# Down projections of two feed-forward layers as seven block products in place of eight, on one Trainium2 core

## The chip, the cores and the metric

The kernel runs on one core of a Trainium2 chip. The core has five engines with queues of their own: TensorE (PE, matmul), VectorE (DVE), ScalarE (ACT), GpSimd (POOL) and SyncE (SP, which here issues the transfers). The metric is the device time of one execution in microseconds (us), as the median of the runs.

## What is computed

A backbone block of two layers over 512 latent tokens (x) and 256 context tokens (ctx), width 1024, in float32. Each layer is attention in three head groups, then a SwiGLU feed-forward with 2816 hidden columns. Layer 1, the last, computes the latent tokens alone. The part that matters, shortened:

```python
def swiglu(h, w1, w3, w2):
    return (jax.nn.silu(h @ w1) * (h @ w3)) @ w2

for layer in range(2):
    last = layer == 1
    ...                                   # modulation mx, mc of c and c_ctx; attention
    x = x + mx[5] * swiglu(modulate(rmsnorm(x, g_ffn[layer]), mx[3], mx[4]),
                           w_ff1[layer], w_ff3[layer], w_ff2[layer])
    if not last:
        ctx = ctx + mc[5] * swiglu(modulate(rmsnorm(ctx, g_ffn[layer]), mc[3], mc[4]),
                                   w_ff1[layer], w_ff3[layer], w_ff2[layer])
return rmsnorm(x, g_final)
```

## The kernel before

Every operation is recorded first (`Plan`, `_Queue`), then a planner lists them by priority and due time and issues them, so that each engine has one fixed order of instructions; all of them carry the line of the issuing call, L375. An operation recorded on `act_dve` or `dve_pool` may go to either of two engines, as the planner decides. `LEAD` says how far ahead weights are asked for, and the buffers of each tag in `SLOTS` set how far ahead they can be: "u" has 39 buffers of 4 KB per partition, for weights, hidden columns, sums and operands alike; "pt" (8) and "s" (7) are the probability and score buffers of attention, "T" is four PSUM buffers of 512 columns and "S" two of a block's up projection.

A float32 matmul is made of three in float32r: each operand is split into a high part (a copy that rounds) and a low part (the operand less its high part), and hi·hi, hi·lo and lo·hi add up in PSUM. For weights `split_w` loads `ws` from HBM and makes `wh` and `wl`.

The feed-forward takes the hidden columns in 22 blocks `ft` of 128. `ff_up` multiplies w1 and w3 of a block with the normalized tokens (hx 512 columns, hc 256): 24 matmuls of 512 columns for each of w1 and w3, and in layer 0 another 24 of 256 columns. ScalarE takes silu of the first into `sg`; `ff_gate` multiplies by the second and splits into `gh` and `gl`. The down projection `ff_down` of block ft - 1 stands between the up parts of block ft: per tile of 128 tokens two halves of 512 output columns with three matmuls each, into two "T" buffers, which DVE adds into the accumulator `y` of that tile (`ys`; six tiles in layer 0, four in layer 1). The last FF_TAIL = 3 blocks are kept back and done after the loop (label ffE), where their products add up in PSUM and go to x through the gate. In layer 0 the loop also carries the modulation of layer 1 (`ada_later`, FF_ADA): DVE operations scalar_tensor_tensor into `acc`, from weights `wa`.

Of the kernel before, what the change touches and what calls it, by code (L numbers as in the profile page):

```python
# [12 lines left out]
F32R = mybir.dt.float32r  # L13
AF = mybir.ActivationFunctionType
ALU = mybir.AluOpType
# [13 lines left out]

ORDER = ["dddd P0 P1 ddddB P2 BABeeeeABAeeeeBABABABeeeeeeeeeCAAAACCCCCC",  # L30
         "P1 P0 B P2 ABBBCAACAABCCCAAB"]
FF_TAIL = 3
FF_ADA = "dddd"
PV_RUN = {"A": 3, "B": 3, "C": 2}
QK_AHEAD = 238
# [3 lines left out]
FT = DFF // 128  # L39
# [339 lines left out]
def dit_block(  # L379
# [8 lines left out]
    plan = Plan(nc, (  # L388
        x, c, ctx_in, c_ctx, w_ada, b_ada, g_attn, g_ffn, w_in, g_q, g_k, lam_q1, lam_k1, lam_q2, lam_k2,
        g_subln, sink_logit, w_out, w_ff1, w_ff3, w_ff2, g_final, k_ident, k_mask, k_ones, k_ropeA, k_ropeB, out))  # L390
    act, dve, pe, pool, sp = (plan.queue(e) for e in ("act", "dve", "pe", "pool", "sp"))
# [14 lines left out]
    def new(tag, shape, name, dt=F32):  # L406
        return plan.tile(pools[tag], [128] + list(shape), dt, tag, nm(name))

    def U(shape, dt=F32, name="u"):
        return new("u", shape, name, dt)  # L410
# [7 lines left out]
    def PT():  # L418
        return new("T", [512], "T")
# [7 lines left out]
    def f(ap):  # L427
        return ap.bitcast(F32)

    def sub(eng, o, a, b):  # L430
        eng.tensor_tensor(o, a, b, ALU.subtract)
# [154 lines left out]
    def ada_later():  # L586
        yield from ada_run(0, (5,), (0, 1))
        yield from ada_run(1, range(2), (0, 1))
        yield from ada_run(1, range(2, 6), (0,))
# [83 lines left out]
    for l in range(2):  # L673
        last = l == 1
# [631 lines left out]
        def ff_gate(hs, sg):  # L1306
            dve.tensor_tensor(sg[:, :ncol], sg[:, :ncol], hs[:, :ncol], ALU.mult)
            gh = new("u", [768], "gh", F32R)
            act_dve.copy(gh[:, :ncol], sg[:, :ncol])
            gl = new("u", [768], "gl", F32R)  # L1310
            sub(dve, gl[:, :ncol], sg[:, :ncol], f(gh[:, :ncol]))
            return gh, gl

        def ff_w2(ft, scale=None):
            def load2(st):
                sp.dma_start(st, w_ff2[l, 128 * ft:128 * ft + 128, :])
            return split_w(load2, [1024], scale=scale)
# [14 lines left out]
        def halves(ap):  # L1332
            return [ap[:, 512 * hf:512 * hf + 512] for hf in range(2)]

        ys, gs, ada = {}, [], ada_later()
        for ft in range(FT):
            plan.label = f"ffn{l}"
            plan.lead = LEAD["else"] if ft == 0 else LEAD["ff"]
            ws = ff_weights(ft)
            down = 0 < ft <= FT - FF_TAIL  # L1340
            w2 = ff_w2(ft - 1) if down else None
            for ch in FF_ADA if l == 0 and 1 < ft < FT - FF_TAIL else "":
                plan.label, plan.lead, ada_eng[0] = "ada1", LEAD["ada"], ch
                next(ada, None)
            plan.label = f"ffn{l}"
            hs = []
            if ft == 0:
                hs = [PS(), PS()]
                for part in (2, 3) if last else (1, 2, 3):
                    for a in range(2):  # L1350
                        ff_up(ws[a], hs[a], part)
            for a in range(2):
                if ft:
                    hs.append(PS())
                s = hs[a]
                for part in range(1 if last else 2):
                    if ft:
                        ff_up(ws[a], s, part)
                    if down:
                        k = 2 * a + part  # L1360
                        for r, i in qtiles[2 * a:2 * a + 2] if last else qtiles[FF_CUT[k]:FF_CUT[k + 1]]:
                            if ft == 1:
                                ys[r, i] = U([1024], name="y")
                            for p, yv in zip(ff_down(gs, [w2], r, i), halves(ys[r, i])):
                                if ft == 1:
                                    act_dve.copy(yv, p)
                                else:
                                    dve.tensor_tensor(yv, p, yv, ALU.add)
                if a == 0:
                    sg = new("u", [768], "sg")  # L1370
                    act.activation(sg[:, :ncol], s[:, :ncol], AF.Silu)
            gs = (gs if ft > FT - FF_TAIL else []) + [ff_gate(hs[1], sg)]
        for _ in ada if not last else ():
            raise ValueError("a part of the modulation is left")
        plan.lead = LEAD["else"]
# [1 line left out]
        gates = [gate_read(l, 1, r) for r in range(1 if last else 2)]  # L1377

        gated = [(slice(512 * hf, 512 * hf + 512), gates[0][hf]) for hf in range(2)] if last else None
        w2s = [ff_w2(ft, gated) for ft in range(FT - FF_TAIL, FT)]  # L1380
        for r, i in qtiles:
            xt = xt0[r, i] = U([1024], name="xf")
            sp.dma_start(xt, xscr[NX * r + i])
            for xv, yv, gate in zip(halves(xt), halves(ys[r, i]), gates[r]):
                dve_pool.tensor_tensor(yv, yv, gate, ALU.mult)
                dve_pool.tensor_tensor(xv, xv, yv, ALU.add)
        if not last:
            hT = new_hT()
        else:
# [90 lines left out]
```

## Time and profile before

| what | value |
|---|---|
| runs | 1730.92, 1727.18, 1730.82 us |
| median | 1730.82 us |
| the profiled execution | 1727.9 us |
| its span | 1726.1 us |
| PE, DVE, ACT, POOL busy | 1677.6, 1189.7, 617.2, 128.9 us |
| granted clock of PE, mean | 0.995 |

The span is what the trace covers; the execution's own time has 1.8 us around it. Busy time is the union of an engine's instructions; matmuls overlap one another in the trace, so the distance between their starts tells more than their length.

### The profile page before, as it was taken

To read this page: it belongs to the slowest core of one execution; us is meant where nothing else is said; L and a number is where in the kernel's file an instruction comes from. 1 tells how busy PE (TensorE), PEld (TensorE's weight loads), DVE (VectorE), ACT (ScalarE), POOL (GpSimd) and SP (SyncE) were. 2 spreads that over 40 slices of the span, in tenths; PEclk is the share of its full clock that TensorE was granted. 3 is DMA by queue.
4 is the path that set the end of the run, shared out by engine and by line. 5 is a ranking of instruction groups with operands and counts; after the bars stand their busy time and mean duration, and the time that the engine had idled before them with its cause. 6 is when DMAs were issued, how large, how long until landed. Compare 5 with 4: busy or idle time off the path is not lost.

```text
span 1726.1 us, 24221 instructions
## 1 busy us (share of the span) xinstructions
PE 1677.6 (97%) x9426; PEld 1367.1 (79%) x9426; DVE 1189.7 (69%) x2036; ACT 617.2 (36%) x1278; POOL 128.9 (7%) x167
## 2 busy tenths in 40 slices
PE   7999898999999999999999999999999999999998
PEld 4787676777888888888888888777777888888886
DVE  3766978576568877676645775787776666666676
ACT  2523877663431212112111153267674411111111
POOL 0230200010000000000000001232000000000010
PEclk9999999999999999999999999999999999999999
DMA  9502230334352555345133251022006632332441
GB/s 322 184 31 85 68 86 1 117 89 120 114 179 86 171 171 168 102 158 164 44 91 117 98 171 37 25 50 50 1 2 164 177 110 74 110 107 77 122 146 49
DMA packets 153278, 182.96 MB, mean 106 GB/s; under 512 B 9316, under 2 KB 121396, under 8 KB 153164
## 3 DMA queue, kind: packets, MB, share of 16 engines
q1 hardware_dynamic: 153164, 181.42, 34.0%
q8 instruction: 74, 1.21, 0.3%
q14 instruction: 40, 0.33, 0.1%
HBM read 163.00 MB, written 9.47 MB: 100 GB/s over the span
## 4 chain that ended last, share of the span: by engine, by line
PE 87%; DVE 5%; ACT 3%; DMA 3%; issue 1%; SPq 1%; POOL 0%; DVEq 0%; POOLq 0%; ACTq 0%
DMA ws__2963<-in_w_out_dram 1%; SPq L375 1%; DMA ws__2951<-in_w_out_dram 1%; PE S__1380 L375 1%; PE S__1379 L375 1%; PE S__1756 L375 0%; PE S__1628 L375 0%; PE S__1561 L375 0%; PE S__1881 L375 0%; PE S__1691 L375 0%; PE S__1823 L375 0%; PE S__1495 L375 0%; PE S__1995 L375 0%; PE S__1993 L375 0%; PE S__1984 L375 0%
## 5 line engine op out<-in xcount | busy, mean ns | idle before, releaser
L375 POOL TENSOR_TENSOR y__1397<-y__1397,gate__1998 128x512 f32<-128x512 f32 x1 | 1.3, 1294 | 481.7 <-DVE y__1397 L375 481.7
L375 POOL TENSOR_TENSOR ws__3494<-ws__3494,gate__3489 128x512 f32<-128x512 f32 x1 | 1.3, 1304 | 292.6 <-DMA ws__3494<-in_w_ff_dram 292.6
L375 DVE TENSOR_TENSOR wl__2186<-ws__2184,wh__2185 128x1024 fp32r<-128x1024 f32 x1 | 1.2, 1224 | 11.6 <-PE T__2121 L375 11.6
L375 ACT ACTIVATE sg__1468<-S__1461 128x768 f32<-128x768 f32 x1 | 0.8, 812 | 21.2 <-PE S__1461 L375 21.2
L375 ACT ACTIVATE sg__1966<-S__1959 128x768 f32<-128x768 f32 x1 | 0.8, 812 | 21.2 <-PE S__1959 L375 21.2
L375 ACT ACTIVATE sg__1860<-S__1853 128x768 f32<-128x768 f32 x1 | 0.8, 812 | 21.2 <-PE S__1853 L375 21.2
L375 ACT ACTIVATE sg__1914<-S__1907 128x768 f32<-128x768 f32 x1 | 0.8, 812 | 21.2 <-PE S__1907 L375 21.2
L375 ACT ACTIVATE sg__1940<-S__1933 128x768 f32<-128x768 f32 x1 | 0.8, 812 | 21.2 <-PE S__1933 L375 21.2
L375 ACT ACT_TABLE_LOAD x6 | 7.7, 1283 | 0.8 <-PEq L1465 0.7
L375 POOL TENSOR_TENSOR ropeG<-ropeA,gqk 128x64 f32<-128x64 f32 (+1 forms) x10 | 6.5, 673 | 5.9 <-DVE gqk L375 5.9
L375 DVE TENSOR_TENSOR sg__1994<-sg__1994,S__1995 128x768 f32<-128x768 f32 x1 | 1.0, 954 | 8.4 <-PE S__1995 L375 8.4
L375 ACT ACTIVATE xn__2033<-xf__2011 128x1024 f32<-128x1024 f32 x1 | 1.1, 1061 | 14.2 <-DVE xf__2011 L375 14.2
L375 PE MATMUL T__115<-wa__116,cstat 128*32 128x128 f32 x8 | 0.7, 417 | 5.6 <-DMA wa__116<-in_w_ada_dram 5.6
L375 ACT ACTIVATE sg__1994<-S__1993 128x768 f32<-128x768 f32 x1 | 0.8, 812 | 14.7 <-PE S__1993 L375 14.7
L375 ACT ACTIVATE sg__3107<-S__3102 128x512 f32<-128x512 f32 x1 | 0.6, 598 | 14.8 <-PE S__3102 L375 14.8
L375 ACT ACTIVATE sg__3195<-S__3190 128x512 f32<-128x512 f32 x1 | 0.6, 597 | 13.9 <-PE S__3190 L375 13.9
L375 ACT ACTIVATE sg__3305<-S__3300 128x512 f32<-128x512 f32 x1 | 0.6, 597 | 13.9 <-PE S__3300 L375 13.9
L375 ACT ACTIVATE sg__3415<-S__3410 128x512 f32<-128x512 f32 x1 | 0.6, 597 | 13.9 <-PE S__3410 L375 13.9
L375 ACT ACTIVATE sg__3129<-S__3124 128x512 f32<-128x512 f32 x1 | 0.6, 597 | 13.9 <-PE S__3124 L375 13.9
L375 ACT ACTIVATE sg__3239<-S__3234 128x512 f32<-128x512 f32 x1 | 0.6, 597 | 13.9 <-PE S__3234 L375 13.9
L375 ACT ACTIVATE sg__3151<-S__3146 128x512 f32<-128x512 f32 x1 | 0.6, 597 | 13.8 <-PE S__3146 L375 13.8
L375 ACT ACTIVATE sg__3261<-S__3256 128x512 f32<-128x512 f32 x1 | 0.6, 597 | 13.8 <-PE S__3256 L375 13.8
(14006 smaller groups left out, 6608.3 us busy)
## 6 DMA issues: line engine op xcount, KB each, us to landing
x__83<-in_x_dram SPq DMA_DIRECT2D x1, 512.0 KB
x__84<-in_x_dram SPq DMA_DIRECT2D x1, 512.0 KB
x__131<-in_x_dram SPq DMA_DIRECT2D x1, 512.0 KB, 5.9
x__136<-in_x_dram SPq DMA_DIRECT2D x1, 512.0 KB, 6.5
x__198<-in_ctx_dram SPq DMA_DIRECT2D x1, 512.0 KB
x__203<-in_ctx_dram SPq DMA_DIRECT2D x1, 512.0 KB
ws__241<-in_w_in_dram SPq DMA_DIRECT2D x1, 512.0 KB
ws__244<-in_w_in_dram SPq DMA_DIRECT2D x1, 512.0 KB
```

The costliest lines, as they stand in the source:

```text
L375: getattr(self.real[op.eng], method)(*args, **kw)
```

## The change

In each layer the blocks 0 to 17 are taken in nine pairs. The hidden columns of a pair (two blocks of 128) and w2's two blocks make a product of 2x2 blocks: the tokens are cut into two halves (384 each in layer 0, 256 in layer 1), the inner dimension into the pair's two blocks, w2's columns into two halves of 512. `wino_down` forms four sums of activations (S) and four of w2 (T) on DVE, splits each operand into high and low parts (`fh`, `fl`), and makes seven products in place of eight, each with an accumulator `yw` per tile of tokens; they stand as a generator between the up parts of the next two blocks. `wino_sum` adds the accumulators up into the four quarters after the loop. 21 accumulators of 2 KB in layer 0 and 14 in layer 1 take the place of six and four `y` of 4 KB; HOMES puts 12 and 10 of them into "pt" and "s" buffers, the others lie in "u". The tail is four blocks in place of three, the gate operations after the loop are on DVE alone, and the multiply by `hs` of a pair's blocks is no longer followed by a split of its own.

```diff
--- before.py
+++ after.py
@@ -29,7 +29,9 @@
 
 ORDER = ["dddd P0 P1 ddddB P2 BABeeeeABAeeeeBABABABeeeeeeeeeCAAAACCCCCC",
          "P1 P0 B P2 ABBBCAACAABCCCAAB"]
-FF_TAIL = 3
+FF_TAIL = (4, 4)
+WINO = (0, 1)
+HOMES = ({'pt': 8, 's': 4}, {'pt': 6, 's': 4})
 FF_ADA = "dddd"
 PV_RUN = {"A": 3, "B": 3, "C": 2}
 QK_AHEAD = 238
@@ -1332,14 +1334,120 @@
         def halves(ap):
             return [ap[:, 512 * hf:512 * hf + 512] for hf in range(2)]
 
+        def split_s(src, shape):
+            hi = U(shape, F32R, "fh")
+            act_dve.copy(hi, src)
+            lo = U(shape, F32R, "fl")
+            sub(dve, lo, src, f(hi))
+            return hi, lo
+
+        spare = []
+
+        def wino_home(form, t):
+
+            for tag, n in HOMES[l].items():
+                if homes.get(tag, 0) < n and (tag != "pt" or form in (1, 5, 6)):
+                    homes[tag] = homes.get(tag, 0) + 1
+                    return new(tag, [512], "yw")
+            if not spare:
+                y = U([2, 512], name="yw")
+                spare.extend((y[:, 1], y[:, 0]))
+            return spare.pop()
+
+        def wino_down(Ge, Go, ft, first):
+
+
+            n = ncol // 2
+            nt = n // 128
+            raws2 = []
+            for k in range(2):
+                w = U([1024], name="w2")
+                sp.dma_start(w, w_ff2[l, 128 * (ft + k):128 * (ft + k) + 128, :])
+                raws2.append(w)
+            we, wo2 = raws2
+            a11, a21, a12, a22 = Ge[:, 0:n], Ge[:, n:2 * n], Go[:, 0:n], Go[:, n:2 * n]
+            b11, b12, b21, b22 = we[:, 0:512], we[:, 512:1024], wo2[:, 0:512], wo2[:, 512:1024]
+
+            def product(form, A, B):
+                (ah, al), (bh, bl) = A, B
+                y = None
+                for t in range(nt):
+                    c = slice(128 * t, 128 * t + 128)
+                    p = PT()
+                    with plan.together():
+                        for k, (a, b) in enumerate(((ah, bh), (ah, bl), (al, bh))):
+                            pe.matmul(p, lhsT=a[:, c], rhs=b, start=(k == 0), stop=(k == 2))
+                    if first:
+                        wino_y[form, t] = wino_home(form, t)
+                        act_dve.copy(wino_y[form, t], p)
+                    else:
+                        dve.tensor_tensor(wino_y[form, t], p, wino_y[form, t], ALU.add)
+
+            def pair(h, j):
+                return h[0][:, j], h[1][:, j]
+
+            sa = split_s(a11, [n])
+            sb = split_s(b11, [512])
+            product(1, sa, sb)
+            yield
+            S, T = U([2, n], name="S12"), U([2, 512], name="T12")
+            dve.tensor_tensor(S[:, 0], a21, a22, ALU.add)
+            sub(dve, T[:, 0], b12, b11)
+            sub(dve, S[:, 1], S[:, 0], a11)
+            sub(dve, T[:, 1], b22, T[:, 0])
+            s12, t12 = split_s(S, [2, n]), split_s(T, [2, 512])
+            S3, T3 = U([2, n], name="S34"), U([2, 512], name="T34")
+            sub(dve, S3[:, 0], a11, a21)
+            sub(dve, T3[:, 0], b22, b12)
+            sub(dve, S3[:, 1], a12, S[:, 1])
+            sub(dve, T3[:, 1], T[:, 1], b21)
+            product(5, pair(s12, 0), pair(t12, 0))
+            yield
+            product(6, pair(s12, 1), pair(t12, 1))
+            yield
+            s34, t34 = split_s(S3, [2, n]), split_s(T3, [2, 512])
+            product(7, pair(s34, 0), pair(t34, 0))
+            yield
+            so2 = split_s(wo2, [1024])
+            so2 = [h.rearrange("p (j n) -> p j n", j=2) for h in so2]
+            product(3, pair(s34, 1), pair(so2, 1))
+            yield
+            sgo = split_s(Go[:, 0:2 * n], [2 * n])
+            sgo = [h.rearrange("p (j n) -> p j n", j=2) for h in sgo]
+            product(4, pair(sgo, 1), pair(t34, 1))
+            yield
+            product(2, pair(sgo, 0), pair(so2, 0))
+            yield
+
+        def wino_sum():
+
+            nt = ncol // 256
+            for t in range(nt):
+                y = [None] + [wino_y[form, t] for form in range(1, 8)]
+                dve.tensor_tensor(y[2], y[1], y[2], ALU.add)
+                dve.tensor_tensor(y[6], y[1], y[6], ALU.add)
+                dve.tensor_tensor(y[7], y[6], y[7], ALU.add)
+                dve.tensor_tensor(y[6], y[6], y[5], ALU.add)
+                dve.tensor_tensor(y[3], y[6], y[3], ALU.add)
+                sub(dve, y[4], y[7], y[4])
+                dve.tensor_tensor(y[7], y[7], y[5], ALU.add)
+                ys[tiles[t]] = [y[2], y[3]]
+                ys[tiles[nt + t]] = [y[4], y[7]]
+
+        homes = {}
+        wino_y, wino, G = {}, None, []
+        tail = FF_TAIL[l]
         ys, gs, ada = {}, [], ada_later()
         for ft in range(FT):
             plan.label = f"ffn{l}"
             plan.lead = LEAD["else"] if ft == 0 else LEAD["ff"]
             ws = ff_weights(ft)
-            down = 0 < ft <= FT - FF_TAIL
+            down = 0 < ft <= FT - tail and l not in WINO
+            if l in WINO and 0 < ft <= FT - tail and ft % 2 == 0:
+                wino = wino_down(*G, ft - 2, ft == 2)
+                G = []
             w2 = ff_w2(ft - 1) if down else None
-            for ch in FF_ADA if l == 0 and 1 < ft < FT - FF_TAIL else "":
+            for ch in FF_ADA if l == 0 and 1 < ft < FT - tail else "":
                 plan.label, plan.lead, ada_eng[0] = "ada1", LEAD["ada"], ch
                 next(ada, None)
             plan.label = f"ffn{l}"
@@ -1366,10 +1474,22 @@
                                     act_dve.copy(yv, p)
                                 else:
                                     dve.tensor_tensor(yv, p, yv, ALU.add)
+                    for _ in range(2 if last else 1):
+                        next(wino, None) if wino else None
                 if a == 0:
                     sg = new("u", [768], "sg")
                     act.activation(sg[:, :ncol], s[:, :ncol], AF.Silu)
-            gs = (gs if ft > FT - FF_TAIL else []) + [ff_gate(hs[1], sg)]
+            if l in WINO and ft < FT - tail:
+                dve.tensor_tensor(sg[:, :ncol], sg[:, :ncol], hs[1][:, :ncol], ALU.mult)
+                G.append(sg)
+            else:
+                gs = (gs if ft > FT - tail else []) + [ff_gate(hs[1], sg)]
+        if wino:
+            for _ in wino:
+                pass
+            wino_sum()
+        else:
+            ys = {k: halves(y) for k, y in ys.items()}
         for _ in ada if not last else ():
             raise ValueError("a part of the modulation is left")
         plan.lead = LEAD["else"]
@@ -1377,13 +1497,13 @@
         gates = [gate_read(l, 1, r) for r in range(1 if last else 2)]
 
         gated = [(slice(512 * hf, 512 * hf + 512), gates[0][hf]) for hf in range(2)] if last else None
-        w2s = [ff_w2(ft, gated) for ft in range(FT - FF_TAIL, FT)]
+        w2s = [ff_w2(ft, gated) for ft in range(FT - tail, FT)]
         for r, i in qtiles:
             xt = xt0[r, i] = U([1024], name="xf")
             sp.dma_start(xt, xscr[NX * r + i])
-            for xv, yv, gate in zip(halves(xt), halves(ys[r, i]), gates[r]):
-                dve_pool.tensor_tensor(yv, yv, gate, ALU.mult)
-                dve_pool.tensor_tensor(xv, xv, yv, ALU.add)
+            for xv, yv, gate in zip(halves(xt), ys[r, i], gates[r]):
+                dve.tensor_tensor(yv, yv, gate, ALU.mult)
+                dve.tensor_tensor(xv, xv, yv, ALU.add)
         if not last:
             hT = new_hT()
         else:
```

**The order of PE,** in layer 1, at the start of a down projection. Names: `T` the PSUM buffer, `wh`, `wl` and `gh`, `gl` the parts of w2 and of the activations, `fh`, `fl` those of the operands of a product. Before, one tile pair of a block:

```order
L375 MATMUL T__3241<-wh__3232,gh__3223 128x512
L375 MATMUL T__3242<-wh__3232,gh__3223 128x512
L375 MATMUL T__3241<-wl__3233,gh__3223 128x512
L375 MATMUL T__3242<-wl__3233,gh__3223 128x512
L375 MATMUL T__3241<-wh__3232,gl__3224 128x512
L375 MATMUL T__3242<-wh__3232,gl__3224 128x512
L375 MATMUL T__3243<-wh__3232,gh__3223 128x512
L375 MATMUL T__3244<-wh__3232,gh__3223 128x512
L375 MATMUL T__3243<-wl__3233,gh__3223 128x512
```

Now, products 1 and 5 of a pair:

```order
L377 MATMUL T__3373<-fh__3371,fh__3369 128x512
L377 MATMUL T__3373<-fl__3372,fh__3369 128x512
L377 MATMUL T__3373<-fh__3371,fl__3370 128x512
L377 MATMUL T__3374<-fh__3371,fh__3369 128x512
L377 MATMUL T__3374<-fl__3372,fh__3369 128x512
L377 MATMUL T__3374<-fh__3371,fl__3370 128x512
L377 MATMUL T__3383<-fh__3379,fh__3377 128x512
L377 MATMUL T__3383<-fl__3380,fh__3377 128x512
L377 MATMUL T__3383<-fh__3379,fl__3378 128x512
L377 MATMUL T__3384<-fh__3379,fh__3377 128x512
L377 MATMUL T__3384<-fl__3380,fh__3377 128x512
L377 MATMUL T__3384<-fh__3379,fl__3378 128x512
```

Each product has three matmuls to a buffer of 512 columns, all of one buffer together, where the two halves of a tile alternated before.

**The order of DVE,** in layer 0, from the gate multiply on in the middle of the modulation's work (blocks 4 and 5). Names: `sg` the activations, `y` and `yw` the accumulators, `acc` the modulation, `w` a block of w2, `S` and `T` without a PSUM operand the sums. Before:

```order
L375 TENSOR_TENSOR sg__1532<-sg__1532,S__1533 128x768
L375 TENSOR_TENSOR y__1408<-T__1536,y__1408 128x512
L375 TENSOR_TENSOR y__1408<-T__1537,y__1408 128x512
L375 TENSOR_TENSOR gl__1541<-sg__1532,gh__1540 128x768
L375 TENSOR_TENSOR y__1411<-T__1538,y__1411 128x512
L375 TENSOR_TENSOR y__1411<-T__1539,y__1411 128x512
L375 SCALAR_TENSOR_TENSOR acc__1557<-wa__1560,cstat,acc__1557 128x1024
L375 COPY cols__1554<-T__1553 128x16
L375 COPY sh_1_1622<-cols__1554 128x16
L375 SCALAR_TENSOR_TENSOR acc__1556<-wa__1587,cstat,acc__1556 128x1024
```

Now:

```order
L377 TENSOR_TENSOR sg__1547<-sg__1547,S__1548 128x768
L377 TENSOR_TENSOR T__1579<-w__1569 128x512
L377 TENSOR_TENSOR S__1578<-sg__1514,sg__1547 128x384
L377 TENSOR_TENSOR T__1579<-w__1570,T__1579 128x512
L377 COPY cols__1561<-T__1560 128x16
L377 TENSOR_TENSOR S__1578<-S__1578,sg__1514 128x384
L377 TENSOR_TENSOR T__1585<-w__1570,w__1569 128x512
L377 CAST fh__1580<-S__1578 128x768
L377 TENSOR_TENSOR fl__1583<-T__1579,fh__1582 128x1024
L377 TENSOR_TENSOR fl__1581<-S__1578,fh__1580 128x768
L377 TENSOR_TENSOR S__1584<-sg__1547,S__1578 128x384
L377 TENSOR_TENSOR T__1585<-T__1579,w__1570 128x512
```

The gate multiply, which ended a block, is followed by sums of S and T and by low parts that the next product waits for; the additions of the block before come after them.

**The order of SP,** in layer 1, loads of w1 and w3 (128x8x128) and w2 (128x1024). Before, two blocks:

```order
L375 DMA ws__3225<-in_w_ff_dram 128x8x128
L375 DMA ws__3228<-in_w_ff_dram 128x8x128
L375 DMA ws__3231<-in_w_ff_dram 128x1024
L375 DMA ws__3247<-in_w_ff_dram 128x8x128
L375 DMA ws__3250<-in_w_ff_dram 128x8x128
L375 DMA ws__3253<-in_w_ff_dram 128x1024
```

Now, one pair:

```order
L377 DMA ws__3287<-in_w_ff_dram 128x8x128
L377 DMA ws__3290<-in_w_ff_dram 128x8x128
L377 DMA ws__3306<-in_w_ff_dram 128x8x128
L377 DMA ws__3309<-in_w_ff_dram 128x8x128
L377 DMA w__3313<-in_w_ff_dram 128x1024
L377 DMA w__3314<-in_w_ff_dram 128x1024
```

The same six loads, with those of w2 side by side behind the others.

## Rows read from the trace of the kernel before

**Rows 1.** The page's engine shares, and its slices of PE and DVE.

```profile
PE 1677.6 (97%) x9426; PEld 1367.1 (79%) x9426; DVE 1189.7 (69%) x2036; ACT 617.2 (36%) x1278; POOL 128.9 (7%) x167
...
PE   7999898999999999999999999999999999999998
...
DVE  3766978576568877676645775787776666666676
```

**Rows 2.** Busy time of each engine by stretch, in us from the start.

```profile
core 0: us, PE busy (x) PEld busy (x) DVE busy (x) ACT busy (x) POOL busy (x), PEclk, DMA share, GB/s
0.00:484.00 484.00, 452.97 (x2960) 349.36 (x2961) 326.29 (x686) 256.81 (x616) 61.35 (x82) 0.99 0.37 116
484.00:1001.00 517.00, 517.00 (x2845) 441.38 (x2844) 355.74 (x442) 90.76 (x106) 3.84 (x3) 1.00 0.38 123
1001.00:1105.00 104.00, 104.00 (x484) 86.28 (x483) 75.84 (x155) 41.80 (x74) 17.72 (x19) 1.00 0.31 97
1105.00:1371.00 266.00, 255.23 (x1607) 201.96 (x1606) 195.65 (x426) 165.36 (x395) 36.12 (x54) 0.99 0.25 64
1371.00:1719.00 348.00, 348.00 (x1538) 288.13 (x1536) 233.52 (x326) 61.74 (x85) 9.28 (x8) 1.00 0.33 102
...
505.00:655.00 150.00, 150.00 (x824) 127.56 (x823) 121.03 (x142) 29.52 (x34) 0.00 (x0) 1.00 0.42 138
```

**Rows 3.** Timeline of PE, layer 0's tail: start, length, tile; 61 such rows between.

```profile
1000.76 0.28 PE L375 MATMUL S__1995<-hc__1281,wl__1992 128*128 128x256 f32 x1
1000.88 0.40 PE L375 MATMUL T__2029<-wh__2003,gh__1974 128*128 128x512 f32 x1
...
1014.96 0.40 PE L375 MATMUL T__2061<-wh__2009,gl__1997 128*128 128x512 f32 x1
```

**Rows 4.** Timeline of PE and DVE, layer 0's loop: neighbours and a last matmul.

```profile
560.28 0.95 DVE L375 TENSOR_TENSOR gl__1477<-sg__1468,gh__1476 128x768 fp32r<-128x768 f32 x1
561.15 1.27 DVE L375 SCALAR_TENSOR_TENSOR acc__1491<-wa__1493,cstat,acc__1491 128x1024 f32<-128x1024 f32 x1
562.35 1.27 DVE L375 SCALAR_TENSOR_TENSOR acc__1490<-wa__1494,cstat,acc__1490 128x1024 f32<-128x1024 f32 x1
...
566.41 0.39 PE L375 MATMUL T__1496<-wh__1485,gl__1477 128*128 128x512 f32 x1
...
566.84 0.69 DVE L375 TENSOR_TENSOR y__1394<-T__1496,y__1394 128x512 f32<-128x512 f32 x1 [2.02 <-PE T__1496 L375]
567.45 0.68 DVE L375 TENSOR_TENSOR y__1394<-T__1497,y__1394 128x512 f32<-128x512 f32 x1
...
574.86 1.22 DVE L375 TENSOR_TENSOR wl__1514<-ws__1512,wh__1513 128x1024 fp32r<-128x1024 f32 x1
575.99 1.22 DVE L375 TENSOR_TENSOR wl__1517<-ws__1515,wh__1516 128x1024 fp32r<-128x1024 f32 x1
```

**Rows 5.** Timeline of SP and PE, layer 1: a w1 load, its use.

```profile
1449.94 0.37 SPq L375 DMA_DIRECT2D ws__3203<-in_w_ff_dram  x1
...
1485.29 0.39 PE L375 MATMUL S__3212<-hx__2966,wh__3204 128*128 128x512 f32 x1
```

**Rows 6.** Timeline of SP, DVE, PE before layer 1's loop: one load.

```profile
1360.28 0.43 SPq L375 DMA_DIRECT2D ws__3045<-in_w_ff_dram  x1
...
1366.92 0.69 DVE L375 CAST wh__3046<-ws__3045 128x1024 fp32r<-128x1024 f32 x1
...
1367.64 1.23 DVE L375 TENSOR_TENSOR wl__3047<-ws__3045,wh__3046 128x1024 fp32r<-128x1024 f32 x1
...
1371.03 0.40 PE L375 MATMUL S__3054<-hx__2966,wh__3046 128*128 128x512 f32 x1
```

**Rows 7.** Timeline at the end: the last matmul and the last transfer.

```profile
1718.99 0.39 PE L375 MATMUL T__3526<-wh__3498,gl__3488 128*128 128x512 f32 x1
...
1722.54 0.33 SPq L375 DMA_DIRECT2D out_dram<-yo__3523  x1
```

## The prediction

> **What bounds the kernel now.** I read the page's engine shares first, then its slices, then a table of stretches, then single rows. TensorE (PE) is busy 97% of the span, VectorE (DVE) 69%, ScalarE 36%, and PE's slices show no hole but at the start and in the middle [rows 1]. [...] The idle time lies in the two attention stretches, which the change leaves alone. So in both feed-forwards a matmul less is its whole step less, for as long as nothing else comes up to the limit; and the engine next to it, DVE, is where the change puts its new work.
>
> **What is removed.** The order of PE has, for the down projections, 1320 matmuls before and 945 + 240 now: nine pairs of blocks per layer, where a pair has 63 instead of 72 matmuls in layer 0 (seven products of three token tiles and three hi/lo terms) and 42 instead of 48 in layer 1, and four blocks in each tail, done as before. That is 81 + 54 = 135 fewer, all 128x128 by 512 columns. The new ones have that same form, so their price is known: 63 in a row, whose first and last start 14.08 us apart, make 14.08 / 62 = 0.227 us each [rows 3]. 135 x 0.227 = **30.7 us**. (The row gives 0.40 us for each; that is its length in the pipeline, not its step.) The tail's row of 24 matmuls per half, 18 before, is work moved from the loop, at no price of its own.
>
> **What is added, on DVE.** Here too the step counts, not the length: between neighbours that wait for nothing a 512-column operation takes 0.61 us of the engine (length 0.69), 768 columns 0.87 (0.95), 1024 columns 1.13 (1.22), the modulation's scalar_tensor_tensor 1.20 (1.27) [rows 4]. Sums of 384 or 256 columns and their low parts are not in the rows; the line through 512 and 1024 gives 0.47 and 0.34, and with 0 and 0.61 as bounds a pair of layer 0, with five of them, is out by at most 0.7 us upward. Per pair of layer 0: removed are three additions from PSUM (1.8), two lows of w2 (2.3), two lows of the gated activations (1.7), together 5.8; added are eight sums (four of 384, four of 512 columns: 4.3) and eight low parts (one of 384 columns, one of 512, three of 768, three of 1024: 7.1); net +5.6. I then summed the rows of DVE's order between every second gate multiply by those steps. Before, the three pairs from block 2 to 7, which also carry layer 1's modulation, come to 122.7 us; the trace has 121.0 of 150 [rows 2], so the steps hold to 1.4%. Now the pairs there have 32.1, 45.2, 47.1 and 41.2 us. PE has 50.0 us for a pair before [rows 2], so 50.0 - 9 x 0.227 = 48.0 now. DVE goes to 94% and 98% in two pairs, against 91% in the fullest of before, and is below 88% in all others of layer 0. In layer 1 the rows from the first to the last gate multiply go from 218.6 to 254.0 us, in a loop that was at 234 of 348 us [rows 2] and gets some 12 us shorter: about 80%.
>
> What hides it: PE's 48 us per pair. What if the cover is thin: four PSUM buffers (SLOTS, T) stand between a product and its addition, and an addition starts 0.43 us after its last matmul starts [rows 4], so a DVE that is behind by more than some three tiles (3 x 3 x 0.227 = 2.0 us) stops PE. In the two full pairs it can fall behind that far at places. Lower bound 0 (DVE below 100% by steps), upper bound by whole lengths instead of steps: 49.7 and 52.1 us against 48.0, so 1.7 + 4.1 = 5.8. I take **+2.5 us**, nearer the steps, since the check against 121.0 speaks for them.
>
> [...]
>
> **The chain at the start of a pair** is new: gate multiply, two sums of S and of T, a high and a low of each, then product 5. In layer 0 PE meanwhile does 24 matmuls of w1's first part, product 1 and 24 of 256 columns (5.4 + 2.0 + 24 x 0.12 = 2.9 us, the step of 256 from [rows 3]), DVE's rows there sum to 6.1: a margin of 4. In layer 1 PE has 32 matmuls, 7.3 us, DVE 4.7: a margin of 2.5. Cost taken as 0. The additions of the seven forms (21 and 14 of 512 columns, 12.7 and 8.5 us) stand beside the four tail blocks' up matmuls (over 10 us of PE each): 0. Six gate and residual operations of GpSimd's move to DVE in the same place, 0.61 us each there: 0.
>
> **Loads.** The bytes are the same, but 21 and 14 accumulators take the place of y and new operands hold "u" buffers, so weights are asked for later. Before, w1 of a block in layer 1 is issued 35.3 us before its first matmul [rows 5]. Now the odd block's w1 goes into a buffer whose last reader stands 72 matmuls before that first use: 72 x 0.227 = 16.3 us, once per pair; in layer 0, 14.4 to 17.6 us. What a load needs from issue to a finished low part: in a burst of nine, 6.64 us to the cast, 10.75 us to the matmul that uses it, with no wait of PE [rows 6]. Margin 3.6 us or more: cost 0. The end after the last matmul, 7.1 us [rows 7], stays.
>
> **Sum.** The profiled execution took 1727.9 us (span 1726.1), 2.9 below the median of the runs, 1730.82, and inside their range of 1727.18 to 1730.92. 1727.9 - 30.7 + 2.5 = 1699.7; the attention of layer 1, where PE idles 10.8 us of 266 [rows 2], may move by 3 us either way as its start is placed anew. Forecast **1700 us**.
>
> **Rivals.**
> *DVE sets the pace in layer 0's full pairs.* For it: 94% and 98%, and a DVE order that is fixed, so an addition whose product is not there holds up everything behind it; in the rows DVE sat idle 29 us of 150, 9.7 per pair. Against it: PE did not wait once there. By whole lengths it costs 5.8 us; with before's idle time kept, 45.2 + 47.1 + 2 x 9.7 - 96.0 = 15.7. In the middle 11: 1697.2 + 11 = 1708 us, in a range of 1703 to 1713.
> *Weights come late (the slower side).* One wait of PE per pair, at the first up matmul of the odd block, because the "u" buffers come free so late. It decides from 30.7 / 18 = 1.7 us per pair, that is, when a load takes 16.3 + 1.7 = 18 us to use. Against it: 10.75 us in the rows of a burst. For it: the queue's loads now come in a burst in each pair. At 19 us, 3 x 18 = 54 us: 1727.9 - 30.7 + 54 = 1751 us. [...]
> *The products are not fewer in effect*: excluded, the order lists them.
>
> **How the numbers follow.** Forecast's case 0.75, with a range of its own of 1696 to 1703; DVE the pace 0.14; weights late 0.08, of which 0.05 slower than before and 0.03 between 1712 and 1736; 0.03 for a slip that I have not thought of. The range of 8 in 10 reaches from 1695 over the DVE case to 1711. A measurement of this kernel can tell about 0.3%, 5.2 us: faster 0.90 (the first two, and most of the rest), same 0.04, slower 0.06.
>
> **What would show it.** Right: about 135 PE rows fewer, PE without idle time in both loops, blocks of layer 1's pairs 6 x 0.227 = 1.4 us shorter, and DVE's busy sum up by some 88 us (906 to 994 by the steps over all rows of its order). DVE the pace: PE idle before products with DVE's additions of yw as releaser, between blocks 3 and 8 alone. Weights late: PE idle before an up matmul S, with wh or wl behind it, once a pair. I am wrong if the two loops together lose less than 24 or more than 34 us, or if attention moves by over 4 us.

## The result, and the profile after

The changed kernel takes 1699.68 us (median of four, 1697.98 to 1702.48) where the kernel before took 1730.64 in the same measurement: a ratio of 0.9827, interval 0.9809 to 0.9846. Timed once more beside a later set of runs it gave 0.9829 (0.9816 to 0.9843). Ratios, here and below, are of the means of the runs; times are medians. The forecast was 1700 us, 1695 to 1711.

The page of the changed kernel, engine shares, and slices of PE and DVE, to hold against [rows 1]:

```profile
PE 1648.1 (97%) x9291; PEld 1343.5 (79%) x9291; DVE 1281.6 (75%) x2189; ACT 695.3 (41%) x1390; POOL 119.4 (7%) x162
...
PE   7999898999999999999999999998999999999998
...
DVE  3766978586576998888768884787877577888896
```

9426 - 9291 = 135 matmuls are gone, PE is as full as it was, and DVE has gained 91.9 us of work. Where the time went is seen when both executions are cut at the same marks: the first up matmul of a layer's feed-forward and its last down matmul. The kernel before, by that cut (layer 0's feed-forward, the attention of layer 1, layer 1's feed-forward; columns as in [rows 2]):

```profile
465.60:1027.00 561.40, 561.40 (x3120) 481.42 (x3119) 390.02 (x502) 116.59 (x146) 7.59 (x8) 1.00 0.41 133
1027.00:1357.40 330.40, 320.32 (x1862) 254.06 (x1861) 239.53 (x524) 184.79 (x433) 50.09 (x68) 0.99 0.21 55
1357.40:1718.99 361.59, 360.89 (x1641) 300.61 (x1639) 241.43 (x342) 68.73 (x98) 9.83 (x9) 1.00 0.35 107
```

The changed kernel by the same cut, then two full pairs of layer 0 and one pair of layer 1, each cut at its first up matmul:

```profile
465.40:1012.56 547.16, 545.16 (x3055) 468.77 (x3054) 445.43 (x590) 157.24 (x203) 2.75 (x5) 1.00 0.42 136
1012.56:1341.90 329.34, 318.69 (x1847) 253.12 (x1846) 234.75 (x515) 181.21 (x425) 48.78 (x68) 0.99 0.21 55
1341.90:1691.21 349.31, 348.61 (x1586) 290.45 (x1585) 283.14 (x415) 109.82 (x161) 6.54 (x7) 1.00 0.37 111
574.56:624.26 49.70, 49.70 (x282) 42.15 (x281) 47.63 (x61) 13.96 (x16) 0.00 (x0) 1.00 0.46 149
624.26:674.87 50.61, 49.89 (x282) 42.08 (x281) 45.45 (x59) 13.33 (x16) 0.00 (x0) 1.00 0.50 160
1445.28:1476.56 31.28, 31.28 (x139) 25.90 (x138) 26.08 (x39) 8.82 (x12) 0.00 (x0) 1.00 0.35 101
```

Layer 1's feed-forward went from 361.59 to 349.31 us: 12.28, and 54 x 0.227 = 12.26. Nothing else shows there; a pair takes 31.28 us with PE full and DVE at 26.08. Layer 0's went from 561.40 to 547.16: 14.24 in place of 81 x 0.227 = 18.4. Of the 4.2 us that are missing, 1.8 are only moved: 16 transposes of 128 columns, 0.11 us each, now stand before the layer's last down matmul and not behind it (the stretch between is 1.1 us shorter). Another 2.0 are waits, all of PE's in that stretch, and 0.4 are left over:

```profile
PE T__2131 L377 <- ACT t__2126 L377: 1.3, 1, 1.3
PE T__1635 L377 <- ACT R__1634 L377: 0.7, 1, 0.7
```

(What waited, for what; us in all, times, longest.) The first stands in the norm behind the tail, the second in a full pair. The timeline around the second, DVE, ACT and PE:

```profile
649.54 1.22 DVE L377 TENSOR_TENSOR fl__1689<-w__1646,fh__1688 128x1024 fp32r<-128x1024 f32 x1
649.71 1.05 ACT L377 CAST fh__1658<-T__1655 128x1024 fp32r<-128x1024 f32 x1 [4.00 <-DVE T__1655 L377]
...
650.66 0.36 ACT L377 COPY R__1634<-T__1633 128x256 f32<-128x256 f32 x1
...
651.08 0.44 PE L377 MATMUL T__1635<-ident,R__1634 128*128 128x128 f32 x2 [0.72 <-ACT R__1634 L377]
```

Layer 1's modulation goes through PE, ScalarE and PE again; its copy `R` stands behind a high part `fh` in ScalarE's order, and that one waited 4.00 us for DVE's sum `T`. So DVE is late here by its sums, but it reaches PE by way of ScalarE and the modulation, not by a product's addition.

### The profile page after: what moved, and what is told of

It reads as the page before. It is cut to its first block, busy times and chain, and to the rows that moved or that the text cites. A ratio compares the mean times of both kernels' runs of the same rounds, so it can differ in the third digit from the quotient of the medians.

```text
span 1698.4 us, 24267 instructions
## 1 busy us (share of the span) xinstructions
PE 1648.1 (97%) x9291; PEld 1343.5 (79%) x9291; DVE 1281.6 (75%) x2189; ACT 695.3 (41%) x1390; POOL 119.4 (7%) x162
## 4 chain that ended last, share of the span: by engine, by line
PE 87%; DVE 5%; DMA 3%; ACT 3%; issue 1%; SPq 1%; DVEq 0%; POOLq 0%; POOL 0%; ACTq 0%
SPq L377 1%; DMA ws__3031<-in_w_out_dram 1%; DMA ws__3043<-in_w_out_dram 1%; PE S__1380 L377 1%; PE S__1379 L377 1%; PE S__1568 L377 1%; PE S__1866 L377 1%; PE S__1790 L377 1%; PE S__1493 L377 1%; PE S__1716 L377 1%; PE S__1933 L377 1%; PE S__2072 L377 0%; PE S__2070 L377 0%; PE S__2061 L377 0%; PE S__2059 L377 0%
## 5 line engine op out<-in xcount | busy, mean ns | idle before, releaser
L377 ACT CAST fh__1997<-sg__1954 128x384 fp32r<-128x384 f32 x1 | 0.5, 514 | 12.7 <-DVE sg__1954 L377 12.7
```

Source lines behind the costliest of these rows:

```text
L377: getattr(self.real[op.eng], method)(*args, **kw)
```

## The experiments

Each ran beside the kernel before; ratios are to that. The table has the three stretches of the profiled executions, cut as above, and PE's idle time in the first.

| kernel | ratio (interval) | layer 0 FF | between | layer 1 FF | idle in layer 0 FF |
|---|---|---|---|---|---|
| before | 1 | 561.4 | 330.4 | 361.6 | 0.0 |
| changed | 0.9827 (0.9809 to 0.9846) | 547.2 | 329.3 | 349.3 | 2.0 |
| changed, again | 0.9829 (0.9816 to 0.9843) | 547.2 | 329.1 | 349.4 | 2.0 |
| pe_only | 0.9823 (0.9808 to 0.9838) | 544.1 | 330.5 | 349.4 | 0.8 |
| eighth_back | 1.0014 (1.0006 to 1.0023) | 565.5 | 331.0 | 361.6 | 2.0 |
| tail4 | 1.0007 (0.9998 to 1.0016) | 564.2 | 331.8 | 361.6 | 0.8 |
| wino0 | 0.9911 (0.9897 to 0.9924) | 546.9 | 328.5 | 361.6 | 1.7 |
| wino1 | 0.9939 (0.9925 to 0.9952) | 564.7 | 330.8 | 349.4 | 1.3 |
| dve_plus4 | 0.9865 (0.9851 to 0.9878) | 552.4 | 330.8 | 349.4 | 5.1 |
| dve_plus8 | 0.9995 (0.9986 to 1.0004) | 557.8 | 328.3 | 366.7 | 9.0 |
| homes_none | 0.9954 (0.9942 to 0.9967) | 565.5 | 328.2 | 349.4 | 12.9 |
| tail42 | 0.9905 (0.9890 to 0.9920) | 546.9 | 327.7 | 357.9 | 1.8 |
| tail22 | 1.0029 (1.0018 to 1.0040) | 558.8 | 339.2 | 358.8 | 12.7 |

**The matmuls alone (pe_only).**

```diff
+            if len(gs) == 1 and drops[0] < 18 * 2 * len(qtiles):
...
+                for hf in range(2):
+                    keep.append((3, 3, 2, 3, 2, 3, 3, 2)[drops[0] % 8])
+                    drops[0] += 1
...
+                            if n < keep[hf]:
+                                pe.matmul(ps[hf], lhsT=gg[:, c0:c0 + 128], rhs=w[:, 512 * hf:512 * hf + 512],
+                                          start=(n == 0), stop=(n == keep[hf] - 1))
```

> The kernel before with 135 matmuls fewer and nothing else: in blocks 0 to 17 the third matmul (low part of the activations by high part of w2) is left out in 3 of every 8 products, 81 in layer 0 and 54 in layer 1; the low part's share of those sums is missing, additions and loads stay. Theory (the gain is 135 matmul steps of TensorE, 0.227 us each): 1730.6 - 30.7 = 1700, ratio 0.982, and some 2 us under the changed kernel, which has two waits of 0.7 and 1.3 us besides. Rival (VectorE's added work costs several us in the full pairs of layer 0, so the steps are worth more than the change shows): below 1696. Rival (a step removed isn't worth a step): above 1705.

0.9823: as much as the whole change, within the intervals. 135 matmuls less, with no other work, are worth some 30 us; nothing larger is hidden behind the change. Its layer-0 stretch is 3.1 us shorter than the changed kernel's, of which 1.2 are waits and most of the rest the moved transposes.

**The eighth product back (eighth_back).**

```diff
-                        for k, (a, b) in enumerate(((ah, bh), (ah, bl), (al, bh))):
+                        terms = ((ah, bh), (ah, bl), (al, bh)) * (2 if form == 2 else 1)
+                        for k, (a, b) in enumerate(terms):
```

> The changed kernel with the eighth product's matmuls put back: product 2 adds its three terms twice, 9 matmuls a pair in layer 0 and 6 in layer 1, 135 in all; VectorE's sums, splits and additions stay as changed, and the result is that with product 2 counted twice. Theory (all the added work of VectorE and ScalarE is hidden): 1699.7 + 30.7 = 1730.4, ratio to the kernel before 1.000 with 0.0015 either way. Rival (the added work costs by itself and eats a part of a larger gain): 1735 or more, ratio above 1.0025.

1.0014, 2.4 us over the kernel before (1.0 to 4.0). Layer 1's stretch is back at 361.6 us to the tenth, with DVE at 284 us in place of 241. In layer 0 the excess is 4.1: PE's idle 1.97, the transposes' 1.8 and a rest of 0.3. Apart from the transposes, the added work costs about what the waits cost. The run also answers a question that the expectation leaves out: PE's new order, with the three matmuls of a buffer in a row, is worth nothing by itself, since as many matmuls take the same 361.6 us in either order.

**The tail alone (tail4).**

```diff
-FF_TAIL = 3
+FF_TAIL = 4
```

> The kernel before with the tail of four blocks in place of three, no pairs. Theory (the matmuls are the same in number, they only move): no change, 1728 to 1733. Rival (fewer additions from PSUM on VectorE, 12 and 8 of 0.6 us, are worth something, or a longer tail lets the end start later or earlier): a move of 3 us or more, ratio outside 0.998 to 1.002.

1.0007, its interval includes 1. The norm's wait, here 0.8 us (`T__2039` for ScalarE's `t__2034`), is there without any pair, and so it is in pe_only (0.8) with the tail of three. It belongs to how the norm falls, not to the products. The moved transposes are there too: layer 0's stretch is 2.7 us longer than in the kernel before. So 2.7 of the 4.2 us that are missing in layer 0 are there without any pair, and the pairs by themselves lose 1.4: 564.2 - 547.2 = 17.0 in place of 18.4, 1.2 of it idle time of PE (2.0 against 0.8).

**One layer at a time (wino0, wino1).**

```diff
-WINO = (0, 1)
+WINO = (0,)        # wino0
+WINO = (1,)        # wino1
```

> The change in layer 0 alone; layer 1 keeps eight products, with a tail of four blocks. Theory: 81 steps less and the two waits that layer 0 got (0.7 and 1.3 us): 1730.6 - 18.4 + 2.0 = 1714, 1712 to 1717. Rival (VectorE sets the pace in layer 0's full pairs): only a small part of the 18.4 arrives, 1720 or more.

> The change in layer 1 alone; layer 0 keeps eight products, with a tail of four blocks. Theory: 54 steps less with nothing against it: 1730.6 - 12.3 = 1718, 1716 to 1720; with the run of layer 0 alone the two gains add up to that of the whole change, 31 us. Rival (one wait for weights per pair): 1 us for each of nine pairs or more is missing, 1727 or more.

0.9911 and 0.9939, 15.4 and 10.5 us on 1729, each with 2.3 either way; together 25.9 where the whole change has 29.6 in its repeated run, a gap at the edge of what these intervals allow. Both also carry the tail of four in the other layer; against tail4 (1.0007) they are 16.6 and 11.8, together 28.4. The stretches are sharper than the ratios: layer 1 has 349.4 in wino1 and 361.6 in wino0, layer 0 546.9 in wino0, and the wait for `R__1634` (0.7) is in wino0 and not in wino1. So the two layers act apart: layer 0's pairs bring 17.3 us against tail4's stretch, of 18.4, and layer 1's bring the whole of theirs.

**More work for DVE (dve_plus4, dve_plus8).**

```diff
             so2 = split_s(wo2, [1024])
+            for _ in range(4):         # 8 in dve_plus8
+                sub(dve, so2[1], wo2, f(so2[0]))
```

> The changed kernel in which the low part of the odd block's w2 (1024 columns) is written five times in place of once: 4 x 1.13 = 4.5 us more of VectorE in each of the 18 pairs, 81 us in all, with nothing else changed and the same result. Theory (VectorE is counted by its steps, and hidden up to TensorE's time for a pair): the three fullest pairs, 46.1, 45.3 and 43.4 us busy in the changed kernel's trace, go to 50.6, 49.8 and 47.9 beside some 49.5 us of TensorE, so +1.5 to +6 us, 1701 to 1706; nothing in layer 1, where 25.4 + 4.5 = 29.9 stand beside 31.3. Rival (VectorE is at its limit in the full pairs already, because operations cost their whole length or because it waits in its fixed order): the three pairs cost all of their 3 x 4.9 us and the others a part, 1715 or more.

> As with four extra writes per pair, but eight: 9.0 us more of VectorE in each pair, 163 us in all. Theory (steps, and the slower of the two engines sets each pair): in layer 0 the five fullest pairs go to 55.2, 54.3, 52.4, 50.5 and 49.6 beside 49.5 us of TensorE, +15; in layer 1 25.4 + 9.0 = 34.4 beside 31.3, 9 x 3.1 = +28; together 1740, 1732 to 1750. Rival (an operation costs its whole length, 0.085 us more each, some 60 a pair in layer 0 and 40 in layer 1): some 60.5 beside 49.5 and 38.3 beside 31.3, 1795 or more.

Four more bring 0.9865, 6.6 us over the changed kernel and at the upper end of the theory: layer 1 nothing (349.4), layer 0 5.2 us. Eight bring 28 us (0.9995), less than the 40 of the theory and far from the 96 of the rival. Three early pairs of layer 1 with eight more, and a late one (columns as in [rows 2]):

```profile
1424.67:1455.95 31.28, 31.28 (x139) 25.91 (x138) 31.25 (x45) 10.18 (x13) 0.00 (x0) 1.00 0.34 99
1455.95:1487.23 31.28, 31.28 (x139) 25.91 (x138) 31.25 (x44) 9.09 (x12) 0.00 (x0) 1.00 0.30 89
1487.23:1518.51 31.28, 31.28 (x139) 25.91 (x138) 31.28 (x43) 10.24 (x14) 0.00 (x0) 1.00 0.29 84
1617.76:1655.15 37.39, 33.92 (x143) 27.29 (x141) 37.13 (x52) 9.98 (x13) 0.08 (x1) 0.95 0.39 119
```

In the first three DVE is busy for 31.25 to 31.28 us of 31.28, and PE still loses nothing. In the third, 42 operations of DVE start, whose lengths add up to 34.28 us. Some of them:

```profile
1491.89 0.42 DVE L377 TENSOR_TENSOR fl__3370<-sg__3331,fh__3369 128x256 fp32r<-128x256 f32 x1
1492.22 1.22 DVE L377 TENSOR_TENSOR fl__3349<-w__3314,fh__3348 128x1024 fp32r<-128x1024 f32 x1
1493.36 0.42 DVE L377 TENSOR_TENSOR S__3381<-sg__3331 128x256 f32<-128x256 f32 x1
1493.69 1.22 DVE L377 TENSOR_TENSOR fl__3349<-w__3314,fh__3348 128x1024 fp32r<-128x1024 f32 x1
1494.83 0.68 DVE L377 TENSOR_TENSOR yw__3191<-T__3354,yw__3191 128x512 f32<-128x512 f32 x1
1495.43 1.22 DVE L377 TENSOR_TENSOR fl__3349<-w__3314,fh__3348 128x1024 fp32r<-128x1024 f32 x1
```

The steps are 0.33 us for 256 columns, 0.60 for 512, 1.14 for 1024: the step is the price, also here, where DVE never rests. The row of 512 columns is 0.68 us long, and in this full queue it costs 0.60. What failed in my expectation was the bill by pairs: a backlog is carried on into the next pair and the tail. By the whole stretch DVE of layer 1 had 349.3 - 283.1 = 66.2 us free, eight more cost 9 x 9.0 = 81, and 81 - 66.2 = 15 against the 17.3 measured. That nearness is partly luck: DVE still had 13.7 us free in that stretch. Of the 17.3, 11.0 are added idle time of PE; the rest are longer steps, some of them at a lower clock (0.95 in the late pair's row). In layer 0 DVE had 101.7 us free for the same 81, and the stretch grew by 10.7 all the same: 8.0 of them in one pair (58.62 us at 628.27, 50.61 in the changed kernel), one of those that carry the modulation. Room in the later pairs was of no use to it.

**Where the accumulators lie (homes_none).**

```diff
-HOMES = ({'pt': 8, 's': 4}, {'pt': 6, 's': 4})
+HOMES = ({}, {})
```

> The changed kernel with all accumulators in 'u' buffers, none in those of probabilities and scores. By the order, a weight in layer 0 is then asked for only 4.8, 7.3, 8.7, 9.1 and 9.3 us of TensorE's work ahead at five places, 11 to 15 at twenty more; in layer 1 the shortest stays at 16.3. In the changed kernel's trace a load is at its cast 4 to 6 us after its issue and needs some 2 us more for its two parts. Theory (a lead above some 8 us costs nothing): waits at two or three places, +3 to +8 us, 1703 to 1708, all in layer 0. Rival (leads of 16 us are short already, weights come late with anything less): 25 waits of 2 to 8 us, 1770 or more. Rival (the buffers are without effect): 1699 to 1701.

0.9954: 22 us over the changed kernel, well beyond the 3 to 8 of the theory, and not near the rival's 70. What the trace shows of it is in layer 0, as expected; layer 1 has 349.4. Of the 18.4 us that layer 0's stretch is longer, 10.9 are added idle time of PE; the rest are longer steps, in part at a lower clock (0.50 behind one of the waits, last section). The expectation went by the lead alone (from issue to first matmul), and that failed: the shortest leads, 6.3 to 7.8 us, cost at most 0.2, and the four longest waits stand behind leads of 8.8 to 9.1. One of the shortest, then one of those four, timeline of SP, ACT, DVE and PE:

```profile
622.83 0.38 SPq L377 DMA_DIRECT2D ws__1595<-in_w_ff_dram  x1
...
626.89 1.05 ACT L377 CAST wh__1596<-ws__1595 128x1024 fp32r<-128x1024 f32 x1 [3.00 <-DMA ws__1595<-in_w_ff_dram]
...
628.07 1.22 DVE L377 TENSOR_TENSOR wl__1597<-ws__1595,wh__1596 128x1024 fp32r<-128x1024 f32 x1
...
671.62 0.38 SPq L377 DMA_DIRECT2D ws__1671<-in_w_ff_dram  x1
...
678.24 1.05 ACT L377 CAST wh__1672<-ws__1671 128x1024 fp32r<-128x1024 f32 x1 [1.89 <-PE S__1660 L377]
...
681.63 1.22 DVE L377 TENSOR_TENSOR wl__1673<-ws__1671,wh__1672 128x1024 fp32r<-128x1024 f32 x1
...
682.90 0.50 PE L377 MATMUL S__1681<-hx__1271,wl__1673 128*128 128x512 f32 x1 [1.91 <-DVE wl__1673 L377]
```

The first took 6.5 us from issue to the end of its low part, the second 11.2, not 8. The first cast was released by its load. The second came 6.6 us after the issue, after 1.89 us in which ScalarE was idle, and was released by a matmul of PE; it reads the loaded weight alone, so it must have waited for the buffer of `wh` (inferred from the releaser; no run varies it). The other three long waits show the same 1.89. The low part then stood 2.3 us behind the cast, in DVE's order behind a cast and three additions. So the lead had to cover here the buffers of the parts and the places in two fixed orders as well as the transfer. Without the part of the change that puts sums into "pt" and "s" buffers, 22 of some 30 us are lost.

**The cover of the final sums (tail22, tail42, and the change again).**

```diff
-FF_TAIL = (4, 4)
+FF_TAIL = (2, 2)        # tail22
+FF_TAIL = (4, 2)        # tail42
```

> The changed kernel with ten pairs per layer and a tail of two blocks: 9 + 6 = 15 matmuls less, 3.4 us of TensorE. What it takes away is cover: the 21 and 14 sums of the forms (12.7 and 8.5 us of VectorE) and the gate operations (2.4 us before the first row can drain a buffer) then stand beside the last two blocks' products and a tail of half the length, and the four PSUM buffers hold 5.4 us of tail products. Theory (the four-block tail is what hides the sums): waits of 4 to 10 us at the end of layer 0's loop and 2 to 6 at that of layer 1, against the 3.4 gained: 1702 to 1712, ratio to the kernel before 0.984 to 0.990. Rival (most sums can be done before product 2, which only one of five needs, so nothing is exposed): 1696, ratio 0.981.

> As with two blocks in both tails, but layer 0 keeps four: 6 matmuls less, 1.4 us. Theory (the sums of layer 1 lose their cover): waits of 2 to 6 us near the end, 1700 to 1704. Rival (nothing exposed): 1698.

> The changed kernel itself, as a partner for the two with shorter tails. Theory: the ratio to the kernel before is again 0.983, 0.981 to 0.985, and the trace shows two added waits of TensorE in layer 0's feed-forward (0.7 and 1.3 us) and none in layer 1's. Rival (the two waits were of that one execution): they are elsewhere or gone, and layer 0's feed-forward differs from 547.2 us by more than 1 us.

Two blocks of tail in place of four cost 34 us (1.0029) and, in layer 1 alone, 12 us (0.9905), although they save 3.4 and 1.4 us of matmuls; I had expected a loss of at most 12 and 4. PE's longest wait in tail22 at the end of layer 0's loop, and in tail42 near the end (what waited, for what; us, times, longest):

```profile
PE T__2166 L377 <- DVE yg__2144 L377: 10.1, 1, 10.1
```

```profile
PE T__3715 L377 <- DVE xf__3696 L377: 7.6, 1, 7.6
```

Direction and place are the theory's, the size is not. I had put 2.4 us of gate operations between the sums and the first addition that empties a PSUM buffer. Timeline of DVE in tail42:

```profile
1681.93 0.69 DVE L377 TENSOR_TENSOR xf__3696<-xf__3696,yw__3196 128x512 f32<-128x512 f32 x1
...
1689.15 0.69 DVE L377 TENSOR_TENSOR xf__3699<-xf__3699,yw__3174 128x512 f32<-128x512 f32 x1
1689.76 0.68 DVE L377 TENSOR_TENSOR xf__3696<-xf__3696,T__3703 128x512 f32<-128x512 f32 x1
```

The first token tile, `xf__3696`, has its gate operations done at 1682.6, but in DVE's fixed order the twelve of the other three tiles, 7.2 us, stand before the addition from `T__3703` that empties the first PSUM buffer. In tail22 sixteen such operations fill the wait. There the attention behind it is also 9.9 us longer; 3.5 of them are added idle time of PE, in waits of up to 1.2 us at the norms, and the rest is not taken apart (the mean granted clock of that stretch is 0.97, in the changed kernel 0.99). The change again has the same two waits (1.3 and 0.7 us), and its layer 0 took 547.2 us once more: they are of the program, not of one execution.

## Why the prediction was right

**The main term.** 135 x 0.227 = 30.7 us: pe_only gains 30.6, eighth_back gives it back, layer 1's stretch shows 12.28 for 12.26. (A row of the tail has 12 matmuls per half, 9 before; the prediction's 24 and 18 are those of a whole tile, and nothing hangs on it.) The bounds named beforehand held: the two loops lost 26.5 us together, and the stretch between moved by 1.1.

**The +2.5 us** has a wrong cause, and the total came out in part by luck. I forecast that DVE's additions would stop PE through the four PSUM buffers in the full pairs, and PE did not wait for an addition's buffer once. Two waits of 2.0 us came, one in a full pair (0.7) by way of ScalarE's copy, the other (1.3) at a norm, where tail4 and pe_only have 0.8 of it without a pair. What the products added is thus some 1.2 us of waits; eighth_back is 2.4 us over the kernel before (1.0 to 4.0) and tail4 1.2, which leaves about as much between them. The luck is in the base: I added the term to the profiled execution of before, 1727.9, which was 2.7 us under the median of 1730.6: from the median the sum is 1702.4 with the term and 1699.9 without, and 1699.68 was measured.

**DVE's bill.** The prediction cut the pairs from gate multiply to gate multiply, and forecast 32.1, 45.2, 47.1 and 41.2 us of DVE, beside 48.0 of PE. The changed kernel by that cut (columns as in [rows 2]):

```profile
501.52:550.32 48.80, 48.80 (x278) 41.50 (x277) 33.08 (x35) 23.87 (x36) 0.00 (x0) 1.00 0.47 151
550.32:599.22 48.90, 48.90 (x278) 41.53 (x277) 45.53 (x57) 12.04 (x16) 0.00 (x0) 1.00 0.47 151
599.22:650.67 51.45, 51.14 (x287) 42.97 (x286) 47.09 (x62) 13.89 (x17) 0.00 (x0) 1.00 0.44 144
650.67:698.52 47.85, 47.44 (x263) 40.77 (x267) 41.01 (x55) 13.85 (x17) 0.00 (x0) 1.00 0.47 154
```

Three pairs of the kernel before, by the same cut:

```profile
506.05:659.36 153.31, 153.31 (x845) 130.63 (x844) 124.57 (x147) 29.52 (x34) 0.00 (x0) 1.00 0.42 137
```

The steps gave DVE's work to 1 us in each pair. PE's time beside it was read wrongly: the 150 us of [rows 2] are not three pairs, which took 153.3, so a pair before is 51.1 us and not 50.0, and the steps' 122.7 belong beside 124.6 and not 121.0 (1.5% low, not 1.4% high). DVE's fullest pairs are at 93% and 92%, where I forecast 94% and 98%. Over the whole its busy time rose by 91.9 us for 88, and in layer 1 it is at 283.14 of 349.31 us (81%) for "about 80%". The rival that took whole lengths (+5.8 us) is refuted as a rule by dve_plus8; the rival's upper end, DVE as the pace, begins where dve_plus4 is: 4.5 us more per pair and 5 us lost.

**The chain at the start of a pair.** Margin forecast in layer 1: 2.5 us. Timeline of the changed kernel, a low part that product 5 needs, and its first use:

```profile
1464.02 0.68 DVE L377 TENSOR_TENSOR fl__3324<-S__3321,fh__3323 128x512 fp32r<-128x512 f32 x1
...
1467.27 0.19 PEld L377 LDWEIGHTS T__3329<-fh__3325,fl__3324 128*128 128x128 f32 x1
```

1467.27 - 1464.70 = 2.57 us, the same in seven pairs. In layer 0 I forecast 4, and the shortest was 2.6.

**Loads.** The leads came as forecast: from issue to first matmul the shortest in the pairs is 16.1 us in layer 1 (16.3 forecast) and 14.3 in layer 0 (14.4), and no wait. But the margin of 3.6 us in layer 0 was not there. SP, ACT, DVE and PE, for the tightest weight:

```profile
560.27 0.38 SPq L377 DMA_DIRECT2D ws__1526<-in_w_ff_dram  x1
...
569.64 1.05 ACT L377 CAST wh__1527<-ws__1526 128x1024 fp32r<-128x1024 f32 x1 [8.34 <-PE T__1518 L377]
...
573.09 1.21 DVE L377 TENSOR_TENSOR wl__1528<-ws__1526,wh__1527 128x1024 fp32r<-128x1024 f32 x1
...
574.56 0.39 PE L377 MATMUL S__1536<-hx__1271,wh__1527 128*128 128x512 f32 x1
...
575.02 0.39 PE L377 MATMUL S__1536<-hx__1271,wl__1528 128*128 128x512 f32 x1
```

The low part ended at 574.30, 0.7 us before its first use at 575.02. I took the 10.75 us of a burst [rows 6] as what a load needs; here it took 14.0. ScalarE was idle for 8.34 us before the cast, and a matmul of PE released it, so, by the same inference as in homes_none, the cast waited for its buffer and not for a place; the low part then stood 2.4 us behind the cast in DVE's order. How much of that a smaller lead would have squeezed out is not shown. The rival "weights late" was nearer than its 0.08 made it look: homes_none has its sign at four places, waits of 1.9 to 2.0 us before an up matmul with `wl` behind them.

**The sums behind the loop** were put at 0 because four tail blocks lie beside them; that term was right, and tail22 shows what it depends on.

## What to carry to other kernels

Where an engine is full, a removed instruction is worth its step between neighbours (here 0.227 us for a matmul whose row is 0.40 long), and the first question about work moved to the next engine is not its share of the span, but its share of each stretch, in steps, with what it can carry over to the next. Buffers and a tail that look like housekeeping can carry the gain: here 22 us hung on where the accumulators lie and 34 on two blocks of tail, against 31 us for the removed matmuls. A weight's lead is to be measured against issue, transfer, the buffers of the parts that are made of it, and its places in every fixed order behind it.

## What was not expected of the hardware

A wait of PE can cost more than its length, here 1.4 us more on one of 1.9. After the wait for `xf__3696` in tail42, PE's steps were nearly twice as long for a while, at a granted clock of 0.50 from 1690.4 to 1694.0 us (timeline of PE):

```profile
1690.49 0.80 PE L377 MATMUL T__3715<-wh__3691,gh__3665 128*128 128x512 f32 x1 [7.59 <-DVE xf__3696 L377]
1691.09 0.63 PE L377 MATMUL T__3715<-wl__3692,gh__3665 128*128 128x512 f32 x1
1691.51 0.63 PE L377 MATMUL T__3715<-wh__3691,gl__3666 128*128 128x512 f32 x1
1691.94 0.63 PE L377 MATMUL T__3715<-wh__3694,gh__3686 128*128 128x512 f32 x1
```

0.43 us from start to start in place of 0.227. In homes_none a lower clock also follows waits of only 2 us, but after two of four like ones: it is 0.65 from 788.0 to 792.6 us, and behind the wait that ended at 682.9 us it is 0.50, and then it is back (columns as in [rows 2]):

```profile
683.80:686.80 3.00, 3.00 (x9) 2.32 (x8) 1.48 (x3) 0.51 (x1) 0.00 (x0) 0.50 0.60 175
686.80:690.00 3.20, 3.20 (x17) 2.72 (x16) 1.27 (x1) 0.00 (x0) 0.00 (x0) 0.97 0.30 59
```

Seven matmuls at 0.43 us cost 7 x 0.2 = 1.4 us more on a wait of 1.9. Shorter waits differ in the changed kernel: those of 0.7 and 1.3 us in layer 0's feed-forward were not followed by it (granted clock 1.00 from 651.0 to 654.0 and from 994.2 to 1000.0 us), and one of 1.16 us in the attention of layer 1 was (0.50 from 1107 to 1110 us). So the length of a wait alone does not tell here what follows it.
